# The first two weight pairs of a hybrid Hyena/gMLP block by eight plain block products instead of seven Winograd products

## The chip, the cores and the metric

One core of a Trainium2 chip runs the whole layer. The metric is the device time of one execution in microseconds; several runs are given by their median. Engines: PE (TensorE, matrix products), DVE (VectorE), ACT (ScalarE), POOL (GpSimd) and SP (SyncE, which here only issues DMAs).

## The reference

One layer of an encoder on x of 2048 x 1024, all float32:

```python
h = rms_norm(x, pre_norm_w)
proj = h @ w_in                                  # 1024 -> 7168
hy_in, hy_gate, sg_u, sg_v, sg_gate = split(proj, [3072, 4096, 5120, 6144])
x0, x1, v = split(short_conv_centred(hy_in, conv_w, conv_b), 3)   # three taps
k = hyena_filter(L, ...)                         # small MLP with sines, decay, l1 norm
y_a = x0 * long_conv_bidir(v * x1, k, skip) * silu(hy_gate)       # FFT convolution
mixed = einsum('hpq,bnqhd->bnphd', sgu_w, layer_norm_per_head(sg_v)) + sgu_b
y_b = sg_u * mixed * silu(sg_gate)
return x + rms_norm(concat([y_a, y_b]) @ w_out, post_norm_w)
```

## The kernel before, in words

**Tiling.** The input projection is done by *pairs* of channel blocks: two blocks of 128 output channels against half of the tokens (1024, `h` = 0 or 1), contracted over 1024 channels. A pair is a 2 x 2 block product of weights (a11, a12, a21, a22) and x (b11, b12, b21, b22), where the second index of x is the token chunk of 512 and the contraction is halved. It is done by the Winograd form of Strassen's scheme, with 7 block products of 12 matmuls each: 4 slices of the contraction, and for each slice three float32r matmuls (high x high, low x high, high x low; `mm3`, L304 to L306) that make up for float32 precision. Every factor is therefore kept split in a high part (rounded by ACT) and a low part (raw minus high, by DVE or POOL).

The factors of x, kept in SBUF as `X[0]` to `X[6]` with [128, high/low, 4 token blocks, 512]: b11, b21, t2, t1, t3, t4, b22, with t1 = b12 - b11, t2 = b22 - t1, t3 = b22 - b12, t4 = b21 - t2. The factors of the weights: a11, a12, s2, s1, s3, a22, s4, with s1 = a21 + a22, s2 = s1 - a11, s3 = a11 - a21, s4 = a12 - s2. Product u multiplies weight factor u by x factor u. A product reads its x factor in all four token blocks.

**Kinds and order.** Pairs are of kind B (gate and u of the gMLP branch), U (x1 and v of the Hyena branch, with a short convolution and a product behind them in `u_job`), G, V, and O for the output projection. `self.order` lists 72 pairs: B(0) (8), U(0) (8), G and V of the first half (12), then U(1), G and V, B(1) of the second half, then O. The weights' sums s1 to s4 of the first 28 pairs are stored to DRAM as split factors (`WS`, named by `SPILL`) when a pair is met first, and read again in the second half (`again`, `self.seen`).

**Stages.** `x_phase` loads x of the first half, norms it (`x_norm`, L443 and L445), transposes it on PE (`x_turn`, L454) and makes the seven factors (`x_sums`, `put`; L496 rounds, L497 subtracts). Then `stream` runs pairs, stage by stage; each stage has pools of its own in the memory of the one before it, and a tile waits for the last reader of the tiles it lies over:

- the tap stage (pool "sg"): pairs 0 to 7, beside them `mlp` (the network for the filter; its first DVE step is L765) and 32 `k1_job`s, which make the filter's taps and transform them (L837 to L865)
- the u stage (pool "fa"): pairs 8 to 15, beside them four `x_job`s, which norm x of the second half and store its factors
- later stages: the filter's transform, the other pairs, the FFT convolution, the output projection.

A background job is a generator; `run` advances all active ones after every second step of the stream, and `background(jobs, rate)` starts `rate` new ones each time. So a stage's background work is spread over its pairs by hand. Within this order a planner of the framework (with a model of costs) sets the order on each engine; engines run in order and wait on semaphores.

**Within a pair** (`stream`): product 0, then products 5 and 6 of the pair before (`finish_pair`), then products 1 to 4. After product 0, 2 and 4 ACT copies the accumulator out (`snap`, L648), and the take classes (`TakeB`, `TakeU`, ...) add the results. The weights of the next pair are loaded by `prep_begin` and split one factor at a time by `prep_unit` (L635 rounds on ACT, L637 subtracts on DVE or POOL; buffers `wu`, five of them; raw weights `wraw`, three). Pair results of [128, 18, 64] or [128, 1024] lie in `wide` buffers, `nw_` of them in a stage.

In `k1_job`, j stands for one of 16 rows, twice (two halves of the channels): two products give the taps, DVE multiplies with the decay (L839), forms sum and difference (`s`, L841 and L842), adds the absolute values to the l1 norm (L844), PE transforms (L862), ACT copies to `ev` (L864) and stores it to `AK` (L865). `s` has four buffers (tag kq, with `wr` and `sk`), `ev` three.

Of the kernel before, what the change touches and what calls it, by code (L numbers as in the profile page):

```python
# [20 lines left out]
D = 1024  # L21
# [224 lines left out]
class Body:  # L246
# [77 lines left out]
    def build(self):  # L324
        with ExitStack() as st:
# [113 lines left out]
    def x_norm(self, xs, xn, pw):  # L439
        nc = self.nc  # L440
        ss = xs.tile([128, 1], F32, name="ss", bufs=2)
        jk = self.junk(xs)
        nc.scalar.activation(jk, xn, AF.Square, accum_out=ss)  # L443
        rs = self.rstd(xs, ss)
        nc.vector.scalar_tensor_tensor(xn, xn, rs, pw, op0=ALU.mult, op1=ALU.mult)  # L445

    def junk(self, xs):
        return self.wide([128, D], "jk") if xs is self.fp else xs.tile([128, D], F32, name="jk")
# [30 lines left out]
    def x_phase(self, xs):  # L479

        nc = self.nc
        pw = xs.tile([128, D], F32, name="pw")
# [9 lines left out]
        self.load_more()  # L492

        def put(u, src, i, eng):
            hi, lo = self.X[u][:, 0, i], self.X[u][:, 1, i]
            nc.scalar.copy(hi, src)  # L496
            eng.tensor_tensor(lo, src, hi.bitcast(F32), op=ALU.subtract)  # L497

        keep = {}
        for i in range(4):  # L500
            with self.tc.high_priority(30):
                self.x_norm(xs, xts[0, i], pw)
            for half in range(2):
                ps = self.x_turn(xts[0, i], half, "ab"[half])
                put(half, ps, i, nc.vector)
                keep[half, i] = xs.tile([128, 512], F32, name=f"b{half}", tag="b", bufs=8)
                nc.scalar.copy(keep[half, i], ps)
        for i in range(4):
            with self.tc.high_priority(30):
                self.x_norm(xs, xts[1, i], pw)  # L510
            raw = lambda n: xs.tile([128, 512], F32, name=n, tag="t", bufs=4)
            self.x_sums(raw, lambda u, src: put(u, src, i, nc.vector if u == 6 else nc.gpsimd), keep[0, i], keep[1, i], xts[1, i])

    def x_jobs(self, h):
# [3 lines left out]
        for i in range(4):  # L518
            yield self.x_job(h, i, pw)

# [125 lines left out]
    def snap(self, ps, tag):  # L646
        s = self.rp.tile([128, 512], F32, name="sn", tag=tag)
# [88 lines left out]
    def mlp(self, mp):  # L736
# [39 lines left out]
        for c in range(2):  # L776
# [3 lines left out]
            for d, src in enumerate((t.rearrange("q (j p) -> q j p", j=4), rev)):  # L780
                hi = mp.tile([128, 4, 128], F32R, name="ghi", bufs=2)
                nc.scalar.copy(hi, src)
                lo = mp.tile([128, 4, 128], F32, name="glo", bufs=2)
# [27 lines left out]
    def k1_weights(self, kp, cs, st):  # L811
# [3 lines left out]
        for d in range(2):  # L815
            wr = kp.tile([128, 512], F32, name="wr", tag="kq", bufs=4)
# [9 lines left out]
    def k1_job(self, kp, cs, st, j):  # L826
# [13 lines left out]
        s = [kp.tile([128, 512], F32, name="s", tag="kq", bufs=4) for _ in range(2)]  # L840
# [4 lines left out]
        if j == 0:  # L845
            sk = kp.tile([1, 512], F32, name="sk", tag="kq", bufs=4)
# [13 lines left out]
        for d in range(2):  # L860
            ps = self.bank("b")
            nc.tensor.matmul(ps, self.ff[:, d], s[d], start=True, stop=True)  # L862
            ev = kp.tile([128, 512], F32, name="ev", bufs=3)
# [306 lines left out]
```

## Time and profile before

| what | value |
|---|---|
| median of 3 runs | 2086.94 us (2083.53 to 2091.46) |
| profiled execution, its own time | 2081.43 us |
| its span | 2079.6 us, mean granted PE clock 0.975 |
| busy share of the span | PE 92%, PE weight load 68%, DVE 65%, ACT 41%, POOL 21% |
| DMA | 515.89 MB, 248 GB/s on average |

The rows of a stage table give, after the length of the stretch, the busy us of each engine and the number of its instructions, the granted clock of PE, the share of time in which the DMA engines worked and the rate. A timeline row is: start, duration, engine, line of the kernel, instruction, written tile <- read tiles, shapes, count, and in brackets the idle time of the engine before it with what ended it. A group row (engine and line) ends with the busy us and the mean in ns of one, and then the idle time before them. A name with q (SPq, ACTq) is the engine's sequencer, which issues DMAs. A matmul's duration reaches into the next one's, so a matmul's cost is read from the distance of two starts. A row of DMA issues ends with the size of one and the us until it has landed; a row of waits gives the total, the number and the longest.

### The profile page before, as it was taken

What the parts mean: (1) busy time and instruction counts of PE and PEld (TensorE: products, weight loads), DVE (VectorE), ACT (ScalarE), POOL (GpSimd) and SP (SyncE); (2) the same over time, 40 slices, a digit from 0 to 9 for tenths busy, and PEclk for the clock granted to TensorE, in tenths of its full rate; (3) what the DMA queues carried; (4) which work ended last, traced back from release to release, by engine and by line L of the source; (5) the groups of instructions that cost most, each with busy time, mean ns of one, the idle gap of its engine ahead of it and who ended that gap; (6) DMA issues with size and microseconds to landing.
All of it is one profiled execution on the core that took longest, in us unless ns stands there. A gap on an engine that the chain in (4) does not pass through costs nothing. (4 is left out here: it accounts for less than half of the span.)

```text
span 2079.6 us, 23943 instructions
## 1 busy us (share of the span) xinstructions
PE 1907.2 (92%) x7832; PEld 1419.1 (68%) x7832; DVE 1347.8 (65%) x2070; ACT 855.0 (41%) x1538; POOL 446.3 (21%) x392
## 2 busy tenths in 40 slices
PE   4689999999999999888999999989999999999997
PEld 3465666777777766666777666656677777887776
DVE  6767878787655545655544888887773226436876
ACT  6344444565434443534444223322322224335443
POOL 3431322233222121111111101101011112323331
PEclk9899999999999999999999999989999999999999
DMA  8388777786779796897786888878978888536563
GB/s 265 110 265 268 238 261 253 227 274 230 247 258 297 259 315 208 327 274 236 256 276 194 294 271 265 282 237 274 302 244 307 282 269 282 194 102 243 192 212 132
DMA packets 330203, 515.89 MB, mean 248 GB/s; under 512 B 107451, under 2 KB 177339, under 8 KB 327359
## 3 DMA queue, kind: packets, MB, share of 16 engines
q1 hardware_dynamic: 263328, 439.58, 64.9%
q10 hardware_dynamic: 61856, 69.81, 9.8%
q0 software_dynamic: 4896, 4.98, 1.0%
q8 instruction: 62, 1.02, 0.2%
q14 instruction: 61, 0.50, 0.1%
HBM read 316.10 MB, written 204.48 MB: 250 GB/s over the span
## 5 line engine op out<-in xcount | busy, mean ns | idle before, releaser
L304 PE MATMUL proj<-x,wu 128*128 128x512 f32 x2016 | 834.9, 415 | 36.0 <-ACT sn L648 15.1
L305 PE MATMUL proj<-x,wu 128*128 128x512 f32 x2016 | 808.2, 401 | 10.6 <-DVE wu L637 8.8
L306 PE MATMUL proj<-x,wu 128*128 128x512 f32 x2016 | 806.6, 400 | 1.2 <-DVE x L559 0.6
L304 PEld LDWEIGHTS proj<-x,wu 128*128 128x128 f32 x2016 | 383.6, 190 | 146.2 <-issue 32.8
L637 POOL TENSOR_TENSOR wu<-wraw,wu 128x512 fp32r<-128x512 f32 x172 | 257.3, 1497 | 1038.1 <-ACT wu L635 855.5
L305 PEld LDWEIGHTS proj<-x,wu 128*128 128x128 f32 x2016 | 383.7, 190 | 113.3 <-issue 24.9
L306 PEld LDWEIGHTS proj<-x,wu 128*128 128x128 f32 x2016 | 383.2, 190 | 94.6 <-issue 12.7
L635 ACT CAST wu<-wraw 128x512 fp32r<-128x512 f32 x216 | 133.5, 619 | 281.6 <-PE proj L306 240.3
L637 DVE TENSOR_TENSOR wu<-ws,wu 128x512 fp32r<-128x512 f32 x176 | 129.7, 739 | 156.0 <-ACT wu L635 155.6
L635 ACT CAST wu<-ws 128x512 fp32r<-128x512 f32 x176 | 108.6, 620 | 220.3 <-PE proj L306 160.3
L648 ACT COPY sn<-proj 128x512 f32<-128x512 f32 x216 | 125.6, 581 | 108.4 <-PE proj L306 80.3
L614 POOL TENSOR_TENSOR ws<-wraw 128x512 f32<-128x512 f32 x44 | 79.0, 1795 | 174.5 <-DVE wu L637 111.7
L1073 DVE TENSOR_TENSOR pa<-b,k 64x512 f32<-64x512 f32 x128 | 87.4, 683 | 40.6 <-PE b L1070 29.8
L614 POOL TENSOR_TENSOR ws<-wraw,ws 128x512 f32<-128x512 f32 x44 | 59.5, 1353 | 223.4 <-DVE wu L637 210.1
L1073 DVE TENSOR_TENSOR pb<-b,k 64x512 f32<-64x512 f32 x128 | 88.8, 694 | 1.8
L614 DVE TENSOR_TENSOR ws<-wraw 128x512 f32<-128x512 f32 x44 | 39.6, 901 | 71.3 <-DMA wraw<-in_w_in_dram 39.2
L1082 PE MATMUL b<-pa,tb 128*128 128x512 f32 x128 | 71.7, 645 | 15.1 <-DVE pa L1077 5.5
L1084 ACT COPY ev<-b 128x512 f32<-128x512 f32 x64 | 37.4, 587 | 99.4 <-PE b L1082 88.8
L559 DVE TENSOR_TENSOR x<-x 128x1024 fp32r<-128x1024 f32 x42 | 56.3, 1381 | 19.2 <-ACT x L558 19.2
L1033 PE MATMUL b<-raw,tk 128*128 128x512 f32 x128 | 62.9, 612 | 5.5 <-issue 4.8
L862 PE MATMUL b<-s,ff 128*128 128x512 f32 x128 | 62.2, 603 | 4.4 <-ACT ev L864 2.9
L1070 PE MATMUL b<-raw,tu 128*128 128x512 f32 x128 | 63.2, 604 | 1.7 <-DMA raw<-AU 1.7
(170 smaller groups left out, 2230.5 us busy)
## 6 DMA issues: line engine op xcount, KB each, us to landing
wraw<-in_w_in_dram SPq DMA_DIRECT2D x84, 512.0 KB, 4.9
WSB<-wu SPq DMA_DIRECT2D x32, 512.0 KB, 4.8
dd<-in_c_dec_dram SPq DMA_DIRECT2D x32, 512.0 KB, 5.6
AK<-ev ACTq DMA_DIRECT2D x64, 256.0 KB, 4.5
WSU<-wu SPq DMA_DIRECT2D x32, 512.0 KB, 4.5
WSG<-wu SPq DMA_DIRECT2D x32, 512.0 KB, 5.0
raw<-AK SPq DMA_DIRECT2D x32, 512.0 KB, 6.9
KF<-ev ACTq DMA_DIRECT2D x32, 512.0 KB, 6.0
```

Of the source, the lines that this page charges most:

```text
L304: t.matmul(ps, sh, mh, start=first, stop=False, **kw)
L305: t.matmul(ps, sl, mh, start=False, stop=False, **kw)
L306: t.matmul(ps, sh, ml, start=False, stop=last, **kw)
L614: eng.tensor_tensor(t, x, y, op=op)
L635: nc.scalar.copy(w[:, 0], src[u])
L637: eng.tensor_tensor(w[:, 1], src[u], w[:, 0].bitcast(F32), op=ALU.subtract)
L648: self.nc.scalar.copy(s, ps)
L862: nc.tensor.matmul(ps, self.ff[:, d], s[d], start=True, stop=True)
L1033: nc.tensor.matmul(ps, tv[:, n], raw[:, n], start=True, stop=True)
L1070: nc.tensor.matmul(u, tv[0][:, n], raw[:, n], start=True, stop=True)
L1073: nc.vector.tensor_tensor(o, uu, kk, op=ALU.mult)
L1082: nc.tensor.matmul(ps, tv[1][:, n], prod[n], start=True, stop=True)
```

## The change

The first two pairs, B(0) with c = 0 and 1, move from `stream` into `x_phase`. They are done by the ordinary eight block products (16 instead of 14 for both): first the two output blocks of token chunk 0 of both pairs, from b11 and b21, then those of chunk 1, from b12 and b22. The plain b12 and b22 are put into the places of t3 and of b22 (`X[4]`, `X[6]`), and the split weights of the second pair lie in the place of t4 (`X[5]`). The second x half is transposed between the products (`turn`), and t1, t2 are written there; t3 and t4 are kept raw and are split into `X[4]` and `X[5]` behind the last product. b11 is kept in buffers of the weights' sums.

The stream then starts at pair 2: the tap stage runs pairs 2 to 9, with two u pairs at its end, and the u stage the six pairs 10 to 15. As the first two pairs no longer make the weights' sums, two new background jobs in the u stage (`w_job`) load their weights again, form s1 to s4, split them and store them to `WS` for the second half. The four DMAs of the second x half that ACT issued go to SP. To make room, `ev` of the tap jobs shares the tag of `s` (five buffers for both, instead of four and three), two tiles of `mlp` share others, and the wide buffers of the tap stage go from three to four. The rate of the u stage's background goes from 0.25 to 0.3.

```diff
-            self.seen = set()
+            self.seen = {p[1:3] for p in self.order[:2]}
...
-                    self.nw_ = 3
+                    self.nw_ = 4
...
-                    self.background(self.x_jobs(1), 0.25)
-                    self.run(self.stream(8))
+                    self.background(self.x_jobs(1), 0.3)
+                    self.run(self.stream(14 - 8))
...
-                xts[c, i] = self.x_load(xs, 0, i, c, 4, nc.scalar if i % 2 else nc.sync)
+                xts[c, i] = self.x_load(xs, 0, i, c, 4, nc.scalar if i % 2 and not c else nc.sync)
...
-                if (c, i) == (0, 3):
-                    self.next_w = self.prep_begin(0)
+                if (c, i) in ((0, 3), (1, 0)):
+                    self.first_weights(c)
...
+        b11 = [self.rp.tile([128, 512], F32, name="b11", tag=t, bufs=n) for t, n in (("ws", 3), ("ws", 3), ("ws", 3), ("s1", 1))]
+        b21 = []
         for i in range(4):
             with self.tc.high_priority(30):
                 self.x_norm(xs, xts[0, i], pw)
             for half in range(2):
                 ps = self.x_turn(xts[0, i], half, "ab"[half])
                 put(half, ps, i, nc.vector)
...
+                if half:
+                    b21.append(xs.tile([128, 512], F32, name="b21", bufs=4))
+                    nc.vector.tensor_copy(b21[i], ps)
+                else:
+                    nc.scalar.copy(b11[i], ps)
+            if i == 1:
+                w = [self.first_split(0, [self.wp.tile([128, 2, 512], F32R, name="wu", tag="wu", bufs=5) for _ in range(4)])]
         for i in range(4):
             with self.tc.high_priority(30):
                 self.x_norm(xs, xts[1, i], pw)
...
+        w.append(self.first_split(1, [X[5][:, :, k] for k in range(4)]))
+        t3 = []
+
+        def turn(i):
+            b12 = self.x_turn(xts[1, i], 0, "a")
+            put(4, b12, i, nc.vector)
+            t3.append(xs.tile([128, 512], F32, name="t3", bufs=4))
+            nc.scalar.copy(t3[i], b12)
+            t1 = xs.tile([128, 512], F32, name="t1", bufs=1)
+            tt(t1, b12, b11[i], op=ALU.subtract)
+            b22 = self.x_turn(xts[1, i], 1, "b")
+            put(6, b22, i, nc.vector)
+            t2 = xs.tile([128, 512], F32, name="t2", bufs=1)
+            tt(t2, b22, t1, op=ALU.subtract)
+            tt(t3[i], b22, t3[i], op=ALU.subtract)
+            tt(b21[i], b21[i], t2, op=ALU.subtract)
+            put(3, t1, i, nc.gpsimd)
+            put(2, t2, i, nc.gpsimd)
+
+        def pair(n, chunk):
+            (b1, b2), c = ((0, 1), (4, 6))[chunk], self.order[n][2]
+            cols = slice(512 * chunk, 512 * chunk + 512)
+            sg, ps = None, None
+            for k in range(2):
+                ps = self.bank("proj")
+                self.product({0: X[b1]}, {0: w[n][2 * k]}, 0, ps, False)
+                yield
+                self.product({0: X[b2]}, {0: w[n][2 * k + 1]}, 0, ps, False, first=False)
+                if k == 0:
+                    sg = xs.tile([128, 512], F32, name="sg", tag="h", bufs=3)
+                    nc.scalar.activation(sg, ps, AF.Silu)
+                else:
+                    ug = xs.tile([128, 512], F32, name="ug", tag="h", bufs=3)
+                    nc.vector.tensor_tensor(ug, ps, sg, op=ALU.mult)
+                    nc.sync.dma_start(self.UG[c][:, cols], ug)
+                yield
+
+        turns = {1: 0, 3: 1, 5: 2, 6: 3}
+        n = 0
+        for p in range(2):
+            for _ in pair(p, 0):
+                if n in turns:
+                    turn(turns[n])
+                n += 1
+        for _ in pair(0, 1):
+            pass
+        self.at = 2
+        self.next_w = self.prep_begin(2)
+        self.prep_unit(self.next_w)
+        for _ in pair(1, 1):
+            self.prep_unit(self.next_w)
+        for u, t in ((4, t3), (5, b21)):
+            for i in range(4):
+                put(u, t[i], i, nc.vector)
...
+    def w_job(self, n):
...
+        for b in self.order[n][3:]:
+            raw.append(self.wide([128, 2, 512], "wr"))
+            nc.sync.dma_start(raw[-1], self.i["w_in"][b].rearrange("p (h k) c -> p h (k c)", h=2))
+        yield
+        yield
...
+        s1 = comb(a21, a22, ALU.add)
+        s2 = comb(s1, a11)
+        s4 = comb(a12, s2)
+        for u, t in ((3, s1), (2, s2), (6, s4)):
+            spill(u, t)
+        spill(4, comb(a11, a21))
...
-        s = [kp.tile([128, 512], F32, name="s", tag="kq", bufs=4) for _ in range(2)]
+        s = [kp.tile([128, 512], F32, name="s", tag="kq", bufs=5) for _ in range(2)]
...
-            ev = kp.tile([128, 512], F32, name="ev", bufs=3)
+            ev = kp.tile([128, 512], F32, name="ev", tag="kq", bufs=5)
```

`first_split` rounds a weight block on ACT (`w[:, 0]`) and takes its low part on POOL; `first_weights` loads the two raw blocks of a pair on SP.

More of the change, by code (lines that the diff above doesn't have):

```diff
@@ L441, in x_norm @@
         ss = xs.tile([128, 1], F32, name="ss", bufs=2)
-        jk = self.junk(xs)
+        jk = self.wide([128, D], "jk") if xs is self.fp else xs.tile([128, D], F32, name="jk")
         nc.scalar.activation(jk, xn, AF.Square, accum_out=ss)
@@ L486, in x_phase @@
             for i in range(4):
-                xts[c, i] = self.x_load(xs, 0, i, c, 4, nc.scalar if i % 2 else nc.sync)
+                xts[c, i] = self.x_load(xs, 0, i, c, 4, nc.scalar if i % 2 and not c else nc.sync)
                 if (c, i) == (0, 0):
                     nc.gpsimd.dma_start(pw, self.i["pre_norm_w"].partition_broadcast(128))
-                if (c, i) == (0, 3):
-                    self.next_w = self.prep_begin(0)
+                if (c, i) in ((0, 3), (1, 0)):
+                    self.first_weights(c)
         self.load_more()
+        X = self.X
+        hi = lambda u, i: X[u][:, 0, i]
+        lo = lambda u, i: X[u][:, 1, i]
         def put(u, src, i, eng):
[L495 to L499, printed above, removed]
+            nc.scalar.copy(hi(u, i), src)
+            eng.tensor_tensor(lo(u, i), src, hi(u, i).bitcast(F32), op=ALU.subtract)
+        b11 = [self.rp.tile([128, 512], F32, name="b11", tag=t, bufs=n) for t, n in (("ws", 3), ("ws", 3), ("ws", 3), ("s1", 1))]
+        b21 = []
         for i in range(4):
@@ new lines, in first_weights, with first_split @@
+    def first_weights(self, n):
+        raw = [self.rp.tile([128, 2, 512], F32, name="wraw", tag="wraw", bufs=3) for _ in range(2)]
+        for t, b in zip(raw, self.order[n][3:]):
+            self.nc.sync.dma_start(t, self.i["w_in"][b].rearrange("p (h k) c -> p h (k c)", h=2))
+        self.first = getattr(self, "first", []) + [raw]
+    def first_split(self, n, out):
+        nc = self.nc
+        for k, w in enumerate(out):
+            src = self.first[n][k // 2][:, k % 2]
+            nc.scalar.copy(w[:, 0], src)
+            nc.gpsimd.tensor_tensor(w[:, 1], src, w[:, 0].bitcast(F32), op=ALU.subtract)
+        return out
@@ new lines, in w_job, with comb, spill @@
+    def w_job(self, n):
+        nc, tt = self.nc, self.nc.vector.tensor_tensor
+        raw = []
+        for b in self.order[n][3:]:
[3 more added lines that the diff above has]
+        yield
+        a11, a12, a21, a22 = [t[:, k] for t in raw for k in range(2)]
+        def comb(x, y, op=ALU.subtract):
+            t = self.f("s")
+            tt(t, x, y, op=op)
+            return t
+        def spill(u, t):
+            hi, lo = self.fsplit(nc.vector, t)
+            for r, part in enumerate((hi, lo)):
+                nc.sync.dma_start(self.WS[self.order[n][1:3]][SPILL.index(u), :, r], part.bitcast(F32))
+        s1 = comb(a21, a22, ALU.add)
[4 more added lines that the diff above has]
+        spill(4, comb(a11, a21))
@@ L519, in x_jobs @@
             yield self.x_job(h, i, pw)
+        for n in range(2):
+            yield self.w_job(n)
     def x_job(self, h, i, pw):
@@ L780, in mlp @@
             for d, src in enumerate((t.rearrange("q (j p) -> q j p", j=4), rev)):
-                hi = mp.tile([128, 4, 128], F32R, name="ghi", bufs=2)
+                hi = mp.tile([128, 4, 128], F32R, name="ghi", tag="arg", bufs=2)
                 nc.scalar.copy(hi, src)
-                lo = mp.tile([128, 4, 128], F32, name="glo", bufs=2)
+                lo = mp.tile([128, 4, 128], F32, name="glo", tag="kk", bufs=2)
                 nc.vector.tensor_tensor(lo, src, hi.bitcast(F32), op=ALU.subtract)
```

13 lines of the change are left out of this document (4 added, 9 removed).

## The prediction

> **What bounds the kernel now.** I read the page first, then a table of stages, then the timelines of single engines around the start, and the waits and groups of the two stages behind it. Nothing after 535 us is touched, so only the first quarter is argued. The table of stages, cut where the work changes (columns: length; busy us of PE, weight load, DVE, ACT, POOL with their instructions; granted clock; DMA share; GB/s):
>
> ```profile
> span 2079.6 us, 23943 instructions
> 0.00:31.20 31.20, 9.70 (x40) 7.74 (x41) 14.61 (x22) 16.47 (x33) 3.87 (x7) 1.00 0.91 250
> 31.20:39.60 8.40, 8.40 (x34) 6.63 (x32) 6.99 (x11) 8.40 (x21) 3.31 (x3) 1.00 1.05 388
> 39.60:59.90 20.30, 3.13 (x18) 2.00 (x17) 17.47 (x20) 10.07 (x19) 20.08 (x13) 0.64 0.64 230
> 59.90:75.50 15.60, 15.03 (x52) 9.98 (x53) 5.05 (x11) 7.00 (x11) 6.93 (x5) 0.81 0.15 41
> 75.50:131.60 56.10, 46.32 (x174) 34.31 (x172) 42.80 (x72) 19.62 (x34) 15.45 (x12) 0.91 0.50 150
> 131.60:352.70 221.10, 201.24 (x717) 135.60 (x718) 176.77 (x233) 102.91 (x160) 54.45 (x55) 0.98 0.82 271
> 352.70:394.90 42.20, 37.53 (x159) 28.39 (x158) 33.06 (x35) 21.88 (x43) 11.73 (x15) 1.00 0.58 186
> 394.90:534.90 140.00, 130.53 (x590) 106.29 (x589) 107.00 (x123) 77.22 (x169) 44.86 (x49) 0.99 0.72 244
> ```
>
> PE sets the pace from 60 us on, at nine tenths busy; the hole is 39.6 to 59.9, where PE works 3 of 20 us and POOL all of it. The timelines of PE and POOL say why:
>
> ```profile
> 31.23 0.78 PE L304 MATMUL proj<-x,wu 128*128 128x512 f32 x1
> 31.81 0.63 PE L305 MATMUL proj<-x,wu 128*128 128x512 f32 x1
> 33.94 0.63 PE L304 MATMUL proj<-x,wu 128*128 128x512 f32 x1
> 40.21 0.63 PE L454 MATMUL a<-ident,xt 128*128 128x128 f32 x4 [0.47 <-issue]
> 59.88 0.79 PE L304 MATMUL proj<-x,wu 128*128 128x512 f32 x1 [13.26 <-ACT x L496]
> 85.45 0.39 PE L305 MATMUL proj<-x,wu 128*128 128x512 f32 x1
> 90.47 0.39 PE L306 MATMUL proj<-x,wu 128*128 128x512 f32 x1
> 37.59 10.00 POOL L497 TENSOR_TENSOR x<-t,x 128x512 fp32r<-128x512 f32 x6 [0.44 <-ACT x L496]
> ```
>
> Products 0 and 1 of the first pair need only the plain blocks of x and run from 31.23 on. Product 2 needs a summed factor of x in all four token blocks, and at 59.88 its first matmul has waited 13 us for the last rounding. Two prices come from here: between 85.45 and 90.47 lie 22 matmuls, 0.228 us each, so a product of 12 costs 2.74 us and a pair of 7 costs 19.2; just after the idle start, 31.81 to 33.94 are 5 matmuls, 0.426 each.
>
> A pair's first product is copied out by ACT (L648); these copies date the pairs:
>
> ```profile
> 74.75 0.58 ACT L648 COPY sn<-proj 128x512 f32<-128x512 f32 x1
> 352.74 0.59 ACT L648 COPY sn<-proj 128x512 f32<-128x512 f32 x1 [0.41 <-ACT ev L864]
> 394.94 0.60 ACT L648 COPY sn<-proj 128x512 f32<-128x512 f32 x1
> 534.86 0.56 ACT L648 COPY sn<-proj 128x512 f32<-128x512 f32 x1
> ```
>
> The first is the copy behind product 4 of pair 0 (five products done); the others are the starts of pairs 8, 10 and 16. Pairs 8 and 9 take 42.2 us, pairs 10 to 15 take 139.9. These two pairs are what the change takes out of the u stage.
>
> **The change, part by part.**
>
> *The first two pairs.* 14 products become 16: +5.5 us of PE. They start where product 0 starts now, 31.2: the same four norms and roundings stand before them, and DVE and ACT have their work of 14 to 31 us exchanged (b21 copies and weight splits for the sums and units of pair 0), not enlarged. 192 matmuls at 0.228 are 43.8 us; about 11 of them at 0.426, +2.2; the transposes still to come between them, some 1.3 us a token block (two groups of 0.63), three blocks, 4. End at 31.2 + 43.8 + 2.2 + 4 = 81.2, if nothing holds PE. What could: the chunk-1 products need x4 and x6 of all four token blocks by 57. Their sources on DVE and POOL:
>
> ```profile
> 11.27 1.28 DVE L445 SCALAR_TENSOR_TENSOR xt<-xt,rs,pw 128x1024 f32<-128x1024 f32 x1
> 37.79 2.32 DVE L445 SCALAR_TENSOR_TENSOR xt<-xt,rs,pw 128x1024 f32<-128x1024 f32 x1
> 44.71 0.68 DVE L497 TENSOR_TENSOR x<-b,x 128x512 fp32r<-128x512 f32 x1
> ```
>
> DVE from 11 to 57: 8 norms at 1.28 to 2.32 (15), 16 lows, 16 sums and differences, 4 copies and 2 products at about 0.68 (26): 41 of 46 us. POOL: 8 weight lows and 8 x lows at 1.67 (ten microseconds for six above), 27 us, against 34 now up to 75.5. ACT, 42 us up to 75.5 now, keeps its 8 norms and 40 copies, 8 of them moved behind the products, and gets two silus with their table loads in exchange. All fit, DVE narrowly; I take no wait. Queues: the four DMAs of the second x half that ACT issues now go to SP, behind two weight loads, and stand in line there with the wait for a raw weight buffer; x arrives a few us later at worst and is needed only at turn 0, so nothing. UG goes out as four DMAs of half the size, after the products: covered by the next pair.
>
> The Trainium skill's page "SBUF — State Buffer", section "Who interferes with whom", speaks against this: a DVE instruction with two SBUF inputs and a GpSimd instruction that reads SBUF lock each other out for a whole instruction. The trace's norm of 1.28 against 2.32 while POOL ran agrees. What it would make of the sum is the third rival below.
>
> *The taps' network (mlp).* Its tiles lie where the x phase's lay, in that order, so they wait for the last readers of t3 and b21. These are now written into x4 and x5 only behind the last products, 71 to 82 us.
>
> ```profile
> 62.82 0.30 DVE L745 MEMSET w<- 128x128 f32 x2
> 72.52 0.59 SPq L753 DMA_DIRECT2D bf<-in_filt_freq_dram  x1
> 75.49 1.52 DVE L765 TENSOR_SCALAR arg<-a,bf 128x512 f32<-128x512 f32 x2
> 131.63 1.29 DVE L839 TENSOR_TENSOR dd<-a,dd 128x512 f32<-128x512 f32 x2 [2.85 <-DMA dd<-in_c_dec_dram]
> ```
>
> Now 12.7 us pass from the memset to the first DVE step of the network, most of it SP issuing sixteen small loads in order; the taps' first step follows 56.1 later. With the memset at 79 the network starts at 92: 16.5 later than now. Bounds: 84 (tiles of the first b21 free at 71 and used at once) and 98 (all loads behind the last write). Between 81.2 and 92 PE does 4 products of pair 2.
>
> *The tap stage.* Now, from 75.5 to pair 8's first copy at 352.7, 277.2 us hold the network, 32 tap jobs and 52 products: 8 pairs less the 5 done, plus one. After the change, from 92 to pair 10's first copy, it is the same network and jobs and 53 products. At the same pace 277.2 + 2.7 = 279.9, so pair 10 starts at 372 against 394.9: 23 us gained. Two things weigh on the pace. First, pairs 8 and 9 are u pairs, with convolutions:
>
> ```profile
> L881 DVE SCALAR_TENSOR_TENSOR t<-rv,cw,t 128x1024 f32<-128x1024 f32 x7 | 13.3, 1898 | 0.1
> L881 DVE SCALAR_TENSOR_TENSOR t<-r,cw,t 128x1024 f32<-128x1024 f32 x7 | 11.9, 1705 | 0.0
> L880 DVE SCALAR_TENSOR_TENSOR t<-r,cw,t 128x1024 f32<-128x1024 f32 x8 | 10.2, 1279 | 3.5 <-ACT edge L884 3.5
> L880 DVE SCALAR_TENSOR_TENSOR t<-rv,cw,t 128x1024 f32<-128x1024 f32 x7 | 9.9, 1420 | 0.0
> L908 DVE TENSOR_TENSOR t<-t,t 128x1024 f32<-128x1024 f32 x7 | 8.5, 1215 | 0.1
> ```
>
> That is 7.5 us of DVE a pair, less the two products of a b pair (1.5): +12 for both, on a DVE busy 177 of 221 us. Between 0 and 12 I take 5, since 44 us of idle DVE lie there but PE waits on it in places. Second, the taps' ev and s tiles, seven buffers now, share five:
>
> ```profile
> 244.17 0.67 DVE L841 TENSOR_TENSOR s<-dd 128x512 f32<-128x512 f32 x1
> 247.45 1.88 PE L862 MATMUL b<-s,ff 128*128 128x512 f32 x4
> 249.31 0.59 ACT L864 COPY ev<-b 128x512 f32<-128x512 f32 x1
> 249.93 0.36 ACTq L865 DMA_DIRECT2D AK<-ev  x1
> AK<-ev ACTq DMA_DIRECT2D x64, 256.0 KB, 4.5
> ACT ev L864 <- DMA AK<-ev: 12.0, 5, 3.0
> ```
>
> An s is held about 5 us (244.17 to 249.33), an ev about 5 (249.31 to 249.93 + 4.5), two of each a job: 20 us of buffer time in a job's 221.1 / 32 = 6.9, so 2.9 of five on average. It fits except in bursts, as the 12 us of waits with three ev buffers already show. A burst blocks DVE at L841, and behind it stand the adds that free PE's banks. From 0 to a job interval longer by 1 us (32 in all); nearest to the waits shown, I take 3. The fourth wide buffer only frees; nothing. Sum: pair 10 at 380, 15 us gained.
>
> *The u stage.* Pairs 10 to 15 are done as now, with more beside them: all four x jobs instead of about three (DVE 2 x 1.5 + 4 x 0.68, 6 us) and two jobs that sum the first pairs' weights for the second half (each 4 sums and 4 lows at 0.68, 5.5; 11 us for both). DVE goes from 107 to 124 of 140 us. ACT +5, on 77. SP issues 4 loads and 16 half-size stores here, instead of 8 stores between 36 and 75 us: about 7 us of an idle queue, 6 MB more against 28% of idle DMA, nothing. These jobs take two of four wide buffers while they wait for their load, which a u pair needs for its convolutions; the add behind that frees a bank of PE. What PE waits for now in this stage:
>
> ```profile
> PE proj L305 <- DVE wu L637: 4.5, 2, 3.4
> ```
>
> Cost between 0 (all in DVE's 33 idle us) and 17 (all of it on the path): 7, as one job falls at the stage's end, where PE already waits, and the other beside the last pair. Below zero nothing: no work leaves these six pairs.
>
> **Sum.** -23 + 5 + 3 + 7 = -8 us. The profiled execution took 2081.4 by its own time (span 2079.6); -8 makes 2073. The median of the runs shown is 2086.9, so in those terms 2079. I count 0.5%, 10.4 us, as what a measurement of this kernel tells from no change; the forecast lies inside it, near its edge.
>
> **Rivals.**
> 1. *Everything hides* (faster). The tap stage keeps its pace and the u stage covers its jobs: -23, 2064. For it: 44 and 33 us of idle DVE in the two stages, and few waits of PE in the latter. Against: DVE works in order, and idle time is not where it is wanted.
> 2. *The taps' five buffers* (slower). Job interval 7.9 instead of 6.9: +32 - 3 over the forecast, 2087 - 8 + 29 = 2108. It decides from 0.1 + (8 + 10.4) / 32, about 0.7 us a job: below that the result is no slower by 0.5%. For it: the waits of ACT on ev with three buffers. Against: 2.9 of five.
> 3. *The shared port* (no change). POOL's 27 us and DVE's 18 of instructions with two SBUF inputs (15 of norms, 4 differences) take turns in the x phase. If DVE waits once its 18 over again, less the 5 spare above, turn 3 ends near 70 and the chunk-1 products start 13 later: 2079 + 13 = 2092. For it: POOL's 20 of 20 us beside a DVE at 17. Against: most DVE work here reads a PSUM operand, and POOL has a fifth less to do. The skill's rule, "SBUF — State Buffer", would have it for every overlap of two such instructions.
> 4. *PE is not filled.* Some factor of x or a weight half comes late as now, and the 16 products end at 97 or later: +16, 2095. The first 8 need nothing that is not ready at 45 us now, which speaks against it.
>
> **How the numbers follow.** Forecast 0.45 (2071 to 2087; 0.18 of it beyond 0.5% faster), rival 1 0.22, rival 2 0.15, rival 3 0.13 (0.02 of it slower), rival 4 0.05 (0.03 slower). Faster 0.18 + 0.22 = 0.40; slower 0.15 + 0.02 + 0.03 = 0.20; the same 0.40. The range goes from a little below rival 1 to a little above rivals 3 and 4, 2060 to 2098; outside are most of rival 2 and the early end of the network's start. The forecast's own range is 2071 to 2087.
>
> **What would show it.** In the changed profile PE should be busy from 31 to about 81 us without a gap over 2 us; the memset of w near 79 and the first network step near 92; the first taps' step near 148; pair 10's first L648 copy near 380 and pair 16's near 527; ev or s waits under 20 us in all. The prediction is wrong if PE idles between 57 and 70 (port), if taps come at over 7.6 us each (buffers), if pairs 10 to 15 take over 155 us (wide buffers), or if the network starts before 84, which would add to the gain.

## The result and the profile after

The changed kernel took 2075.32 us (median of 6 runs, 2069.44 to 2079.52) against 2084.71 (6 runs, 2082.41 to 2091.46) in the same comparison: a ratio of 0.9948, 95% interval 0.9930 to 0.9967. The profiled execution of after took 2079.52 us, the slowest of its six; that of before took 2081.43. So the two profiles differ by 2 us where the medians differ by 9, and what they show is where time moved rather than the whole gain.

The table of stages of after (columns as before). It is cut at the times of before up to 59.9, then near the end of the sixteen products, at the first step of the taps and at the starts of pairs 10, 16 and 18:

```profile
0.00:31.20 31.20, 12.10 (x47) 9.98 (x48) 17.36 (x26) 20.06 (x42) 10.43 (x11) 1.00 0.89 230
31.20:39.60 8.40, 8.40 (x39) 6.96 (x38) 7.66 (x10) 6.83 (x13) 5.64 (x5) 1.00 0.66 222
39.60:59.90 20.30, 20.30 (x103) 17.06 (x103) 17.41 (x24) 9.65 (x18) 12.42 (x9) 1.00 0.86 282
59.90:76.20 16.30, 16.30 (x74) 13.49 (x73) 7.93 (x12) 6.76 (x13) 1.77 (x2) 1.00 0.54 191
76.20:142.20 66.00, 57.49 (x237) 43.58 (x235) 45.94 (x82) 24.55 (x43) 23.72 (x15) 0.95 0.51 154
142.20:365.20 223.00, 202.80 (x734) 137.81 (x735) 182.70 (x236) 109.44 (x179) 52.54 (x63) 0.98 0.81 266
365.20:518.40 153.20, 131.36 (x563) 102.26 (x563) 118.39 (x136) 79.45 (x170) 43.03 (x48) 0.94 0.72 248
518.40:572.60 54.20, 44.68 (x165) 32.33 (x164) 30.52 (x36) 25.02 (x49) 11.12 (x11) 0.87 0.86 287
```

The hole is gone: PE works 20.30 of 20.30 us from 39.6 to 59.9. The last of the sixteen products ends at 75.9, pair 2's first follows at once, and PE has no pause before 108.8. The last two rows are the bad news. Pairs 10 to 15 take 153.2 us instead of 140.0 with nearly the same busy time of PE (131.36 against 130.53), and pairs 16 and 17, whose own work the change does not touch, take 54.2. The same two pairs before:

```profile
534.90:572.70 37.80, 37.00 (x152) 27.99 (x151) 24.61 (x27) 19.14 (x39) 11.61 (x11) 1.00 0.85 288
```

The copies that date pairs 2, 10, 16 and 18 in the timeline of ACT after (L753 is L648 of before), and pair 18 before:

```profile
78.82 0.59 ACT L753 COPY sn<-proj 128x512 f32<-128x512 f32 x1 [2.10 <-PE proj L306]
365.18 0.59 ACT L753 COPY sn<-proj 128x512 f32<-128x512 f32 x1 [0.40 <-ACT ev L969]
518.36 0.58 ACT L753 COPY sn<-proj 128x512 f32<-128x512 f32 x1
572.58 0.58 ACT L753 COPY sn<-proj 128x512 f32<-128x512 f32 x1
```

```profile
572.68 0.58 ACT L648 COPY sn<-proj 128x512 f32<-128x512 f32 x1
```

Pair 10 starts 29.8 us earlier than before (394.94), pair 16 16.5 earlier (534.86), pair 18 0.1 earlier. Everything won by pair 10 is given back by pair 18: 13.3 us in pairs 10 to 15 and 16.4 in pairs 16 and 17. The waits of PE in the u stage and the two pairs behind it, after and then before (us in total, times, longest):

```profile
PE proj L304 <- DVE r L757: 13.6, 3, 7.5
PE b L1138 <- DMA raw<-AK: 3.9, 1, 3.9
PE proj L304 <- ACT wu L740: 3.7, 1, 3.7
```

```profile
PE proj L305 <- DVE wu L637: 5.3, 3, 3.4
```

Where they lie, in the timeline of PE after:

```profile
26.91 0.79 PE L304 MATMUL proj<-x,wu 128*128 128x512 f32 x1 [0.72 <-ACT x L498]
116.59 0.77 PE L304 MATMUL proj<-x,wu 128*128 128x512 f32 x1 [7.73 <-DVE ug L178]
510.48 1.32 PE L304 MATMUL proj<-x,wu 128*128 128x512 f32 x2 [7.54 <-DVE r L757]
537.73 1.32 PE L304 MATMUL proj<-x,wu 128*128 128x512 f32 x2 [5.59 <-DVE r L757]
545.12 3.75 PE L1138 MATMUL b<-raw,tk 128*128 128x512 f32 x4 [3.93 <-DMA raw<-AK]
```

Two of the waits lie in pairs 16 and 17, 5.59 and 3.93 us, and they are nearly all of PE's idle time there (54.20 - 44.68). Each of the DVE waits is an add (or product) that frees a bank of PE and stands late in DVE's order. Ahead of 537.73, DVE worked nearly without a break on convolutions, on lows and sums of the second sum job (L299, L602) and on weight sums and lows, and reached the add at 536.91:

```profile
523.37 1.28 DVE L299 TENSOR_TENSOR lo<-s,hi 128x512 fp32r<-128x512 f32 x2
524.57 0.68 DVE L602 TENSOR_TENSOR s<-wr 128x512 f32<-128x512 f32 x1
...
529.28 1.78 DVE L299 TENSOR_TENSOR lo<-s,hi 128x512 fp32r<-128x512 f32 x1
530.98 1.27 DVE L986 SCALAR_TENSOR_TENSOR t<-r,cw,t 128x1024 f32<-128x1024 f32 x1
...
536.91 0.68 DVE L757 TENSOR_TENSOR r<-proj,sn 128x512 f32<-128x512 f32 x1
```

The wait for a load, before 545.12, is tied to the same lateness: on SP's queue the first load of `raw` (539.07) stands behind the store of a convolution's product (537.01), on which DVE works from 535.77 on.

### The profile page after: what moved, and what is told of

The parts are those of the page before. It is cut to its first block, busy times and chain, and to the rows that moved or that the text cites. A ratio compares the mean times of both kernels' runs of the same rounds, so it can differ in the third digit from the quotient of the medians.

```text
span 2077.7 us, 24006 instructions
## 1 busy us (share of the span) xinstructions
PE 1908.6 (92%) x7856; PEld 1420.4 (68%) x7856; DVE 1350.8 (65%) x2082; ACT 854.3 (41%) x1534; POOL 438.8 (21%) x384
## 4 chain that ended last, share of the span: by engine, by line
PE 35%; DVE 6%; DMA 6%; issue 3%; ACT 1%; POOL 1%; SPq 0%; ACTq 0%; DVEq 0%; POOLq 0%
PE proj L304 8%; PE proj L306 8%; PE proj L305 8%; PE b L1187 3%; PE b L1213 3%; PE b L1175 2%; DMA WT<-t 1%; DMA tb<-in_c_tv_dram 1%; DMA wraw<-Y 1%; DVE pb L1178 1%; DMA x<-WT 1%; DVE pa L1178 1%; PE a L1219 1%; DVE pa L1182 1%; PE b L1102 1%
## 5 line engine op out<-in xcount | busy, mean ns | idle before, releaser
L306 PEld LDWEIGHTS proj<-x,wu 128*128 128x128 f32 x1992 | 379.5, 191 | 91.6 <-issue 12.7
L742 DVE TENSOR_TENSOR wu<-ws,wu 128x512 fp32r<-128x512 f32 x168 | 123.7, 740 | 153.0 <-ACT wu L740 152.6
L740 ACT CAST wu<-ws 128x512 fp32r<-128x512 f32 x168 | 103.6, 620 | 244.2 <-PE proj L306 189.5
L753 ACT COPY sn<-proj 128x512 f32<-128x512 f32 x210 | 122.1, 581 | 114.3 <-PE proj L306 83.9
L719 POOL TENSOR_TENSOR ws<-wraw 128x512 f32<-128x512 f32 x42 | 70.6, 1681 | 143.0 <-DVE wu L742 100.5
```

The lines of the kernel that those rows point to most:

```text
L306: t.matmul(ps, sh, ml, start=False, stop=last, **kw)
L719: eng.tensor_tensor(t, x, y, op=op)
L740: nc.scalar.copy(w[:, 0], src[u])
L742: eng.tensor_tensor(w[:, 1], src[u], w[:, 0].bitcast(F32), op=ALU.subtract)
L753: self.nc.scalar.copy(s, ps)
```

## The experiments

Diffs are against after. Dates are of the profiled execution of each kernel; "10-15" and "16-17" are the us that these pairs took. Each kernel is compared with runs of before of its own group, whose median is 2079.65 for after again, the raw blocks, the jobs left out and the tap buffers; 2081.59 for the two rates, the convolutions and the early tiles; 2084.40 for the sums on POOL, the stores on ACT and the late network; 2079.92 for the last one.

| kernel | pair 10 | 10-15 | 16-17 | pair 18 | median us (range) | ratio to before [95%] |
|---|---|---|---|---|---|---|
| before | 394.9 | 139.9 | 37.8 | 572.7 | 2079.65 to 2084.71 | |
| after | 365.2 | 153.2 | 54.2 | 572.6 | 2075.32 (2069.44-2079.52) | 0.9948 [0.9930, 0.9967] |
| after again | 367.5 | 152.6 | 54.7 | 574.9 | 2074.79 (2070.67-2082.02) | 0.9979 [0.9964, 0.9994] |
| raw blocks in xt | 363.1 | 144.5 | 53.2 | 560.7 | 2064.77 (2061.38-2065.92) | 0.9927 [0.9908, 0.9947] |
| no sum jobs | 366.9 | 146.1 | 39.5 | 552.5 | 2057.62 (2051.27-2065.05) | 0.9901 [0.9875, 0.9926] |
| tap buffers back | 366.6 | 151.7 | 54.2 | 572.6 | 2077.50 (2066.55-2082.34) | 0.9989 [0.9972, 1.0007] |
| rate 0.4 | 368.4 | 157.8 | 45.7 | 571.8 | 2070.89 (2065.09-2079.38) | 0.9951 [0.9937, 0.9965] |
| xt and rate 0.4 | 364.9 | 156.0 | 44.1 | 565.0 | 2066.80 (2059.25-2081.55) | 0.9942 [0.9923, 0.9961] |
| no convolutions | 359.5 | 150.8 | 53.2 | 563.5 | 2059.92 (one run) | |
| early tiles | 367.6 | 152.9 | 54.5 | 575.0 | 2074.70 (2068.58-2082.21) | 0.9975 [0.9961, 0.9989] |
| xt, sums on POOL | 364.8 | 146.9 | 58.0 | 569.7 | 2075.99 (2070.70-2083.84) | 0.9961 [0.9939, 0.9982] |
| xt, stores on ACT | 369.0 | 145.9 | 49.0 | 563.9 | 2068.49 (2065.45-2070.17) | 0.9922 [0.9895, 0.9949] |
| late network | 359.5 | 150.7 | 58.6 | 568.8 | 2071.61 (one run) | |
| late network, no jobs | 362.7 | 143.1 | 37.7 | 543.5 | 2064.69 (2052.58-2071.95) | 0.9911 [0.9879, 0.9943] |

**After again**, unaltered.

> The changed kernel once more, unaltered. Its first profile has pair 10 start at 365.2 us, pair 16 at 518.4 and pair 18 at 572.6 (before: 394.9, 534.9, 572.7): 30 us gained up to the end of the tap stage, all of it back by pair 18, and yet the runs differ by 9 us in the median. Theory: the gain up to pair 10 and the loss behind it are set by the order on the engines, so pairs 10, 16 and 18 stand within 3 us of these values again, and what varies between executions lies later. Rival: the loss between pairs 10 and 18 is itself a matter of the single execution; then pair 18 moves by 5 us or more.

The gain came out at 0.2% here (12 runs against 23, medians 4.9 us apart) and 0.5% in the first comparison (six against six, 9.4 us). Pair 18 is dated within 2.3 us of the first profile, as the theory had it, so dates up to there can be compared to some 3 us.

**The raw blocks of the sum jobs in the buffers of the u stage's x tiles** (tag xt) instead of the wide buffers, which a u pair's convolutions need:

```diff
-            raw.append(self.wide([128, 2, 512], "wr"))
+            raw.append(self.fp.tile([128, 2, 512], F32, name="wr", tag="xt", bufs=2))
```

> The raw weights of the two weight-sum jobs lie in the buffers of the x tiles of the u stage instead of two of the four wide buffers; all else as changed. Theory (wide buffers): PE's waits of 7.5 and 5.6 us on the add r of a u pair go, with the slow clock behind them; pairs 10 to 16 take about 142 us instead of 153, pair 18 starts at 553 to 560, and the time is 8 to 16 us under the changed kernel, ratio to before 0.987 to 0.991. Rival (DVE's work of these jobs, 11 us): the waits stay or move, pair 18 starts at 568 or later, ratio 0.994 to 0.996.

Pairs 10 to 15 came down from 153 to 144.5 us, and the pause of 7.5 us before 510.48 is not among its waits: the longest left in the stage is 3.0 us on a weight. So the wide buffers were the larger part of the 13 us. Pair 18 came at 560.7, at the late end of what the theory had, and the ratio, 0.9927, between the two: pairs 16 and 17 stayed at 53. In place of the wait on the add, two others stand there in its timeline of PE:

```profile
522.42 0.80 PE L304 MATMUL proj<-x,wu 128*128 128x512 f32 x1 [5.81 <-ACT sn L753]
529.05 0.80 PE L304 MATMUL proj<-x,wu 128*128 128x512 f32 x1 [3.27 <-ACT wu L740]
```

**The sum jobs left out**; the second half's first two B pairs form the sums themselves, beside its products, and do not store them:

```diff
-            self.seen = {p[1:3] for p in self.order[:2]}
+            self.seen, self.fresh = set(), {p[1:3] for p in self.order[:2]}
...
-        for n in range(2):
-            yield self.w_job(n)
...
-        if u in SPILL and not again and key[0] != "O":
+        if u in SPILL and not again and key[0] != "O" and key not in self.fresh:
```

> The two weight-sum jobs are left out of the u stage; the second half's first two pairs load their raw weights in full and form the sums themselves, unstored. Theory (the jobs are what gives the gain back): pairs 10 to 18 take about 178 us as in the kernel before, pair 18 starts at 540 to 550; the second half's first two pairs cost 0 to 4 us each more; ratio to before 0.984 to 0.990. Rival (the denser x jobs, rate 0.3, and the convolutions of pair 9 do it): pair 18 starts at 560 or later, ratio 0.992 to 0.997.

Both places recover: 146.1 and 39.5 us, the second close to before's 37.8. PE is busy 38.71 of 39.5 us and the granted clock is 1.00, where after had 0.87:

```profile
513.00:552.50 39.50, 38.71 (x156) 28.73 (x155) 25.20 (x27) 20.19 (x40) 12.13 (x11) 1.00 0.88 299
```

So all but some 2 us of the loss in pairs 16 and 17, and half of that in pairs 10 to 15, is that of the two jobs. The other half, 6.2 us, stays without them; the denser x jobs and pair 9's convolutions are left for it, and no run takes these apart. Pair 18 came 2.5 us later than the theory's range. The price in the second half is higher than expected: its first two B pairs (48 and 49) take 76.4 us instead of 62.8. But the twelve pairs ahead of them take 399.9 instead of 411.0, so that the way from pair 18 to pair 71 is no longer than after's (1467.9 against 1471.8 us); why those twelve are faster was not tried. In the medians this version beats both kernels, and its interval lies clear of that of after again.

**The tap stage's buffers as before** (ev three of its own, s four, wide three):

```diff
-                    self.nw_ = 4
+                    self.nw_ = 3
...
-        s = [kp.tile([128, 512], F32, name="s", tag="kq", bufs=5) for _ in range(2)]
+        s = [kp.tile([128, 512], F32, name="s", tag="kq", bufs=4) for _ in range(2)]
...
-            ev = kp.tile([128, 512], F32, name="ev", tag="kq", bufs=5)
+            ev = kp.tile([128, 512], F32, name="ev", bufs=3)
```

> The taps' ev and s tiles apart again, three and four buffers, and the tap stage's wide buffers back to three, so that it fits. Theory (the shared five do not bind: the tap stage keeps its pace, 279 us from the network's first step to pair 10): pair 10 within 3 us of 365.2, time as the changed kernel within 4 us. Rival (my forecast's terms, 3 us for the buffers and more in bursts, hidden by something else that got faster): pair 10 at 355 to 361. If three wide buffers bind with two u pairs in the stage, pair 10 is later than 368.

Pair 10 at 366.6, between the two profiles of after: the five buffers cost nothing that can be seen. The run takes back the fourth wide buffer too, and a gain on one side could hide a loss on the other. The waits of after for a buffer of ev or s to be stored, in the tap jobs' stretch, speak against that, 1.9 us in all:

```profile
DVE s L947 <- DMA AK<-ev: 1.6, 1, 1.6
```

```profile
ACT ev L969 <- DMA AK<-ev: 0.3, 1, 0.3
```

**The u stage's background at rate 0.4**, alone and with the raw blocks in xt, so that the second job ends ahead of the stage:

```diff
-                    self.background(self.x_jobs(1), 0.3)
+                    self.background(self.x_jobs(1), 0.4)
```

> The u stage's background jobs start at a rate of 0.4 instead of 0.3, so the second weight-sum job falls beside the last pairs and not behind them; its raw weights stay in the wide buffers. Theory (two losses: the wide buffers, about 9 us within pairs 10 to 15, and the second job's place at the end of the stage, 14 us in pairs 16 and 17, where the next pair's tiles and raw weights stand behind its stores): pairs 16 and 17 take 38 to 44 us instead of 54, pairs 10 to 15 keep 150 to 165 us; pair 18 starts 5 to 15 us before 574, the time falls by 3 to 12 us under the changed kernel. Rival (both losses are the wide buffers): pairs 16 and 17 gain no more than 6 us and pairs 10 to 15 lose it again.

> Both cures: raw weights of the weight-sum jobs in the x buffers, and the rate 0.4. Theory: pairs 10 to 15 take 142 to 148 us and pairs 16 and 17 38 to 44; pair 18 starts at 545 to 555 as without the jobs (552.5), and the time is 14 to 22 us under the changed kernel. Rival (DVE's work of the jobs costs by itself, 11 us): pair 18 at 560 or later.

Pairs 16 and 17 gain 9 us (45.7 and 44.1), and pairs 10 to 15 lose half of it again at rate 0.4 alone (157.8 instead of 153) and more than all of it with xt (156.0 where xt alone has 144.5). An earlier job mostly moves the loss. Pair 18 at 565.0 falls to the rival of the second forecast, that DVE's work of the jobs costs by itself; the runs with the sums on POOL and the stores on ACT below were made for that.

**The short convolutions and the product of the first two u pairs left out** (`u_job` stores the sums as they are):

```diff
+        nc.vector.memset(self.edge, 0.0)
...
+        if h == 0 and c < 2:
+            nc.sync.dma_start(self.U0[c], r1[:, 1:17].rearrange("q j p -> q (j p)"))
+            return
```

> The short convolutions and the product behind the first two u pairs of the first half are left out (their raw result is stored instead), so the tap stage has 15 us less of DVE work; the output misses these two convolutions. My forecast took 5 us for the convolutions in the tap stage, and the trace of the changed kernel shows the stage no slower than before. Theory (DVE's spare time covers them): pair 10 starts within 3 us of 366. Rival (they do cost, and something else got faster by as much): pair 10 at 355 to 362.

Pair 10 at 359.5, 5.7 to 8.0 us earlier than with them. The row of the tap jobs, to be set against 142.20:365.20 above:

```profile
142.20:359.50 217.30, 200.40 (x722) 135.10 (x721) 171.95 (x228) 102.36 (x159) 53.70 (x56) 0.98 0.82 274
```

PE idles 16.9 us in it, against 20.2 after and 19.9 before: 3.3 of the 5.7 us are idle time of PE. So the convolutions do cost, as the rival had it, in this one execution.

**The tiles that the network waits for allocated first in the x phase**, so that it starts earlier:

```diff
+        b21s = [xs.tile([128, 512], F32, name="b21", bufs=4) for _ in range(4)]
+        t3s = [xs.tile([128, 512], F32, name="t3", bufs=4) for _ in range(4)]
```

> The raw b21 and t3 tiles are put first in the x phase's memory, so that the taps' network no longer lies over them and can start before the sixteen products end, at 60 to 75 us instead of 86; nothing else is changed. Theory 1 (the tap stage is a chain of the network and 32 jobs beside a PE with slack; its length of 279 us goes with the network's start): pair 10 moves up by the same 11 to 26 us, to 340 to 355. Theory 2 (PE-bound: the stage's length is PE's work and its pauses): pair 10 moves up by less than 5 us, as the same products still have to be done behind it.

It tells nothing of what an earlier network would bring, and decides neither theory, since the network did not move: its first DVE step stood at 87.0, against 86.2 and 86.8. The last readers of these tiles do not set that date alone; what does was not tried further.

**With xt, the sums and lows of the jobs on POOL**, and **with xt, their stores on ACT's queue**:

```diff
-        nc, tt = self.nc, self.nc.vector.tensor_tensor
+        nc, tt = self.nc, self.nc.gpsimd.tensor_tensor
...
-            hi, lo = self.fsplit(nc.vector, t)
+            hi, lo = self.fsplit(nc.gpsimd, t)
```

```diff
-                nc.sync.dma_start(self.WS[self.order[n][1:3]][SPILL.index(u), :, r], part.bitcast(F32))
+                nc.scalar.dma_start(self.WS[self.order[n][1:3]][SPILL.index(u), :, r], part.bitcast(F32))
```

> As the kernel with the raw weights in the x buffers, and the weight-sum jobs' 16 sums and lows run on POOL instead of DVE. There pairs 10 to 17 take 198 us, without the jobs 186. Theory (the rest of the jobs' price is DVE's work, about 11 us on an engine at nine tenths): pair 18 starts at 548 to 554 and pairs 16 and 17 take under 45 us. Rival (it is the eight stores and the raw loads behind them on SP's queue at the end of the stage): pairs 16 and 17 still take 50 us or more, the more so as POOL is slower.

> As the kernel with the raw weights in the x buffers, and the weight-sum jobs' 16 stores are issued by ACT instead of SP. Theory (DVE's work): pairs 16 and 17 stay at 50 us or more, pair 18 at 558 to 563. Rival (SP's queue): the raw weights of the next pairs are loaded 5 us earlier, pairs 16 and 17 take 40 to 46 us, pair 18 at 548 to 554.

With the work taken off DVE, pairs 16 and 17 became longer, 58.0 instead of 53.2. So it is not enough to take load off DVE; and since the same sums then come later, from POOL, the run does not show that DVE's load costs nothing. The timeline of ACT of this kernel, and then of PE, show what PE waited for:

```profile
525.63 0.62 ACT L297 CAST hi<-s 128x512 fp32r<-128x512 f32 x1 [0.73 <-POOL s L602]
530.50 0.62 ACT L297 CAST hi<-s 128x512 fp32r<-128x512 f32 x1 [4.26 <-POOL s L602]
531.03 0.58 ACT L753 COPY sn<-proj 128x512 f32<-128x512 f32 x1
...
538.40 1.14 ACT L740 CAST wu<-wraw 128x512 fp32r<-128x512 f32 x2 [4.71 <-DMA wraw<-in_w_in_dram]
```

```profile
531.66 0.80 PE L304 MATMUL proj<-x,wu 128*128 128x512 f32 x1 [9.57 <-ACT sn L753]
539.07 0.80 PE L304 MATMUL proj<-x,wu 128*128 128x512 f32 x1 [4.06 <-ACT wu L740]
```

The copy of a pair's first product stands in ACT's order behind a rounding of the job (L297), which waits for the job's sum; PE waits 9.57 us for that copy. The second wait is for a raw weight, whose load SP issues at 533.35, behind the last of the job's stores (532.50). With the stores on ACT, SP issues the two raw weights that xt alone loads at 522.43 and 523.12 already at 504.70 and 513.61, and the two pairs take 49.0 us, 4.2 less than with xt alone. That lies between what the two theories had, so these stores ahead of the loads on SP's queue are one part of it. That the order on ACT and DVE is the rest is argued from the waits; no run shows it alone.

**One pair of the stream ahead of the network**, the other seven beside the tap jobs at rate 1.6:

```diff
+                    self.run(self.stream(1))
...
-                        self.background(self.k1_jobs(kp), 1.4)
-                        self.run(self.stream(8))
+                        self.background(self.k1_jobs(kp), 1.6)
+                        self.run(self.stream(7))
```

> The taps' network is put behind the first pair of the tap stage instead of beside it (jobs at a rate of 1.6, so that they still fit the other seven pairs); nothing else is changed. The network starts 15 to 20 us later, at 101 to 107. Theory 1 (chain: the stage's length goes with the network's start): pair 10 starts 12 us or more later, at 378 to 388. Theory 2 (PE-bound): pair 10 stays below 371, as PE does a pair more before the network and a pair less behind it.

The network starts 5 us later (91.5), the taps 7 later (149.0), and pair 10 comes 6 to 8 us earlier. So the start of the network does not set the end of the tap stage; the network was to come 15 to 20 us later, and the higher rate of the jobs was changed with it, so the test is weaker than planned. A part of the reason shows between pair 2's first copy and the end of the long pause of after, in the rows of after and of this kernel:

```profile
78.80:116.60 37.80, 30.07 (x125) 21.80 (x124) 29.81 (x55) 12.81 (x23) 16.21 (x6) 0.95 0.35 118
```

```profile
78.70:118.00 39.30, 36.35 (x148) 26.17 (x146) 29.28 (x48) 13.53 (x23) 14.53 (x7) 1.00 0.38 128
```

PE does 36.35 us of work instead of 30.07. After has its pause of 7.73 us there: the product `ug` (L178), which frees a bank, stands behind the network's steps:

```profile
110.55 3.69 DVE L875 SCALAR_TENSOR_TENSOR arg<-kk,arg 128x512 f32<-128x512 f32 x6
...
115.77 0.68 DVE L178 TENSOR_TENSOR ug<-proj,sg 128x512 f32<-128x512 f32 x1
```

With a pair ahead of the network, that product comes at 94.59, between two of its steps. Before had a pause of 5.1 us of the same sort at 104.29. It is not the whole reason: from pair 2 to pair 10 PE idles 27.0 us here and 28.7 in after, so most of the 7.7 us comes back as idle time further on, and what the higher rate did was not tried alone.

**Late network and no sum jobs together.**

> The taps' network begins one pair later (one pair of the stream runs before it, the tap jobs start at rate 1.6 over seven pairs) and the two background jobs for the sums of the first pairs' weights are left out (the second half forms these sums itself, with its pairs). Theory (the u stage's wide buffers and the handover to the next stage are lost to these jobs; the later network keeps PE supplied, without its pause of 7.7 us on the product behind the network's DVE steps): pair 10 near 360 as with the late network alone, pairs 10 to 15 in 146 and pairs 16 and 17 in 39.5 as without the jobs, so pair 18 near 546 and the median near 2057.6 - 6 = 2052. Rival (the 6 us of the late network are not kept: what PE does earlier, the loads of the u stage or the stores in front of it take back, as the 30 us up to pair 10 were taken back): pair 10 near 360, pair 18 at 552 as without the jobs alone, median 2058.

Pair 18 starts at 543.5, 29 us ahead of both kernels and 9 ahead of "no sum jobs" alone: up to there the theory held, with 2.5 us to spare. The median did not follow: 2064.69, 7 us above that of "no sum jobs", where the theories had 2052 and 2058. The two intervals overlap, so which is the better cannot be told. In the profiles the 9 us are lost again in stages that neither edit touches: 9.6 us in pairs 18 to 27 (292.0 against 282.4), and 8.2 in pairs 28 to 35, here of after, of "no sum jobs" and of this kernel:

```profile
860.20:1112.40 252.20, 223.33 (x1003) 177.00 (x1002) 140.50 (x214) 112.75 (x216) 40.41 (x41) 0.97 0.80 252
```

```profile
834.90:1084.40 249.50, 223.33 (x1003) 177.03 (x1002) 140.40 (x214) 112.56 (x216) 40.25 (x41) 0.97 0.81 256
```

```profile
835.50:1093.20 257.70, 226.36 (x996) 180.80 (x995) 139.29 (x221) 111.77 (x217) 39.48 (x41) 0.94 0.80 252
```

The last has a granted clock of 0.94 and PE work 3 us longer. From pair 18 to pair 71 "no sum jobs" took 1467.9 us and this kernel 1488.9, with the same work but not in the same order: behind pair 18 DVE takes the add of the pair first in the one (557.45), and two weight sums ahead of it in the other (551.13 and 552.77). After took 1471.8 and 1472.0, and 1458.9 with the tap buffers back. So the spread may come from the order behind pair 18, or from the single execution; one profile of each kernel does not tell which.

## Why the forecast's number held, step by step

The forecast of 2079 against a measured 2075.3 is right in its sum and not in its terms, which were off in ways that cancel. None of the four signs of being wrong came up (pairs 10 to 15 at 153 us were nearest, with 155 as the limit), and the gain that the sum describes was all the same gone at pair 18. So the number was in good part luck.

- *The first two pairs.* The end of the 16 products was put at 81.2; it came at 75.9. PE's first matmul of a product stood at 26.91, not at 31.2; the length, 50 us forecast, was 49.0. That the start would not move was what failed here: the work of 14 to 31 us was counted as exchanged, and what of it made the start earlier was not tried. No pause: rival 4 fell.
- *The shared port* (rival 3) would have held the chunk-1 products by 13 us. PE has no idle time from 31.2 to 76.2, beside a DVE at 17.41 and a POOL at 12.42 of 20.3 us. Single instructions were longer: of the eight norms, the four that began beside a POOL instruction took 1.51 to 2.23 us, the four others 1.27 or 1.28, some 2.6 us more in all. So the Trainium skill's rule, "SBUF — State Buffer", section "Who interferes with whom", fits the single instructions here and cost PE nothing: the rival had the mechanism right and its size and place wrong.
- *The network* was to start at 92 and started at 86.18, still 10.7 later than before:

```profile
78.20 0.31 DVE L850 MEMSET w<- 128x128 f32 x2
86.18 1.67 DVE L870 TENSOR_SCALAR arg<-a,bf 128x512 f32<-128x512 f32 x2 [0.53 <-PE a L866]
```

  The memset was near its 79, but only 8.0 us passed from there instead of the 12.7 of before. The 12.7 had been read as SP's sixteen loads in order; but in after the step runs before SP issues the last of them (88.40), and in before it stood behind a weight low that waited for ACT:

```profile
74.88 0.69 DVE L637 TENSOR_TENSOR wu<-ws,wu 128x512 fp32r<-128x512 f32 x1 [6.42 <-ACT wu L635]
```

  An offset between two events was taken for the length of a chain. The taps followed 56.0 later, as forecast (56.1).
- *The tap stage* took 279.0 us from the network's start to pair 10, where 279.9 + 5 + 3 stood. The 5 for the convolutions were about right (5.7 to 8.0, in one execution); the 3 for the buffers were nothing that can be seen, and rival 2 fell with them. Some 6 us more are gone that no run here accounts for. That the stage is a chain from the network's start, on which the 372 rested, does not agree with the late network, where a later network came with an earlier pair 10; its rate was changed too, so this is not proved alone. Pair 10 came at 365.2 and not at 380.
- *The u stage* cost 13.3 instead of 7, within its bound of 17. The wide buffers were named as what could go wrong and put at no price of their own; they were some 8 of the 13. That the rest of the work beside the pairs is covered is not shown: without the jobs the six pairs still take 6.2 us more than before.
- *Behind the u stage* nothing was forecast, and 16.4 us were lost: the step of the forecast that failed worst. "One job falls at the stage's end" was said, and its price was sought in DVE's idle time. It was paid in the next two pairs: in after by an add of DVE and a load behind a store that waited for DVE, and with xt by a copy of ACT and a raw weight of SP, all of which stand behind the job or beside it in the orders of their engines.

By dates: 14.8 us better than forecast at pair 10, 6.3 worse in the u stage, 16.4 worse in the two pairs behind it: 7.9 worse at pair 18, where the profiles stand even. The medians differ by 9.4 us all the same, or by 4.9 with more runs; that part is found in no stage of the two profiles and stays open. It may lie behind pair 18: before's one profile takes 1473.7 us from there to pair 71, and twelve of the thirteen profiles with the change take less, 1458.9 to 1472.4. Why was not tested. Rival 1, that everything hides, had 372 for pair 10, nearer to 365.2 than the forecast, and was wrong behind it; "no sum jobs" is what it looks like, 22.0 us under before in the same comparison, where rival 1 had 23.

## What to carry to other kernels

A background job that is spread over a stage by hand must be costed at the stage's end: what is left of it stands ahead of the next stage's first adds, copies and loads on the engines and queues that work in order, and the idle time of an engine, summed over the stage, told nothing of that price here. A job that borrows a buffer of the foreground while it waits for a load costs what the foreground would have done with it, so give it another tag first (here 8 us for one line). And before work is moved to make a sum for later, try the version that makes it anew where it is used: it had the lowest median of the kernels here whose output is whole, though its interval overlaps those of xt and of the late network without jobs.

## What the runs showed of the chip

Two things had not been expected. The granted clock stood lower where PE had paused: 0.87 in pairs 16 and 17 of after, and 1.00 in the same pairs before and without the sum jobs. Of the 16.4 us lost there, PE's idle time accounts for 8.7 (54.20 - 44.68 against 37.80 - 37.00); its busy time grew by 7.7, of which the 13 further matmuls make about 3 at 0.23 us. The rest goes with the clock, and it lies behind the two pauses that end at 537.73 and 545.12:

```profile
537.70:549.60 11.90, 7.94 (x14) 4.36 (x15) 1.51 (x3) 4.21 (x7) 0.48 (x3) 0.50 0.76 257
549.60:572.60 23.00, 23.00 (x92) 16.90 (x91) 10.02 (x12) 11.20 (x23) 3.90 (x5) 1.00 0.94 297
```

The granted clock is 0.50 in the first row, and matmuls start 0.43 us apart (538.85 and 539.28) instead of 0.23. So these pauses were followed by more than their own length; that a pause causes the lower clock was not tested. And on one core the same work behind pair 18, in another order, took 21 us more (1467.9 and 1488.9), some of it with the granted clock (0.97 and 0.94 in pairs 28 to 35), while the two profiles of after agree on pair 18 within 2.3 us: an edit of the first quarter is better read from those dates than from the whole time.
